# Later, separate plane transposes, feature-major sample outputs, one activation table set and six raw buffers in a streaming-encoder step

## The chip, the cores and the metric

The kernel runs on one core of a Trainium2 chip. The metric is the device time of one execution in microseconds, the median of several runs. The core has a matrix engine (TensorE, PE in the profile; its weight loads are shown apart as PEld), a vector engine (DVE), a scalar engine for activations and copies (ACT), a general engine (POOL) and a sync engine (SP) that here only issues transfers. Each engine works through its own instructions in a fixed order and waits for others by semaphores.

## The reference

One layer of a streaming encoder runs for two groups of rows that share all weights: 256 new positions of a prompt stream, and 64 new positions of a sample stream that has 256 cached positions. D_MODEL is 2048.

```python
xn = rmsnorm(x, norm_mix)
q, k, v, u, vs, g = split(xn @ w_in)            # 8 heads x 128 for q, k, v; 8 groups x 128 for u, vs
# attention, per head and query block, keys of all earlier positions:
z = q @ k.T * 128 ** -0.5
log_stay = where(mask, log_sigmoid(-z), 0)
w = where(mask, exp(log_sigmoid(z) + reverse_cumsum(log_stay) - log_stay), 0)
a = w @ v
bb = gelu(u) * (w_spatial . rmsnorm(gelu(vs)) + b_spatial)
merged = sigmoid(g_a) * (a @ w_branch_a) + sigmoid(g_b) * (bb @ w_branch_b)
h = x + merged @ w_out
y = rmsnorm(h + (silu(gate) * up) @ w_down)     # gate, up = rmsnorm(h) @ w_gate_up, width 5632
```

The outputs are y, the new k and v rows of both groups, and the normalised vs rows of the sample group, all in float32.

## The kernel before

All activations are kept with features on the 128 partitions and the 320 positions (256 prompt, 64 sample) side by side in the free dimension, so one weight tile of 128 by 128 serves both groups. Each float32 product is made of three matmuls in the faster fp32r type (`product`, lines 79 to 84): high half of the weight by high half of x, high by low, low by high. So each weight tile that arrives from HBM is split: `halved` (lines 66 to 72) has ACT cast the raw tile to the high half `wh` (L69) and DVE subtract to get the low half `wl` (L70). Four split tiles (`wsplit`) and three raw tiles (`wraw`) of 128 by 1024 rotate. A call of `weights` (lines 74 to 77) issues one raw transfer of 512 KB on SP's queue and splits it. `block` (lines 86 to 97) makes one output tile of 128 features from all weight tiles of its column, eight k-slices per raw tile, and calls `tick()` after each raw tile: a tick is 24 matmuls.

Work beside the products is put in by ticks: `at(t, fn, p)` runs `fn(p)` when tick t is reached while the program is being written out. A planner then orders the instructions of each engine by this order as priority and by its own estimate of when each is ready; an instruction that it thinks ready early can move ahead on its engine. `tc.keep_in_program_order(ins)` pins one instruction behind whatever was written for its engine just before it. SP's order in the first stage is written by hand.

The stages, in order:

1. Heads 0 and 1 of q, k, v are made k-slice by k-slice, while x is still arriving (lines 169 to 212). Step s needs slices of x from the pair transfers `load_x` (L174) and two raw tiles, one per head, from `load_w` (L178). The raw tiles of this stage lie in a pool of ten, `rpool`, whose memory goes to the attention's pool `apool` afterwards. The normalisation factor `rx` is applied to the results.
2. Heads 2 to 7, six ticks each, k first, then q, then v. Attention runs for a pair of heads at a time, beside these products and those of vs. `attend(p, now)` (lines 380 to 386) sets its steps:
   - `att_scores` (now+1): TensorE makes scores in three PSUM banks of the four `aux` ones; DVE and ACT bring them to the tile `w`; ACT computes Abs, Exp and Ln into `e`, in two parts (L298 to L300).
   - `att_values` (now+1): `turn_begin` splits v into its two planes of 16 bits with four ACT copies (L266, L267) and has ACT issue one DMA transpose (L269).
   - `att_sums` (now+2): DVE does the reverse sums (L307, L311, L313).
   - `att_weights` (now+3): ACT computes Exp on `w` (L318), then for each of the two 16-bit planes a copy (L323) and a DMA transpose on its own queue (L324), from `e` to `c`.
   - `att_join` (now+5): DVE writes the two turned planes together again (L331), and the planes of v (`turn_end`, L277).
   - `att_out` (now+8): TensorE multiplies weights and values (L343 to L351). The prompt's outputs come with features on partitions. The sample's come with positions on partitions, so ACT copies them (`own`, L347) and TensorE transposes them (L353). Then ACT and DVE split the outputs into high and low halves (L357, L358).
   The tiles `w`, `e` and `c` exist once each, so a pair's scores can be written only when the pair before is through with them.
3. vs (eight blocks, Gelu), u (eight blocks), with the spatial gate's steps, which use the same `turn_begin` and `turn_end`.
4. Gates, branch products, w_out, the feed-forward network in three slices, and the last normalisation. The change does not touch these, apart from the first block of gates, up to which the raw tiles of stage 2 are used.

Of the kernel before, what the change touches and what calls it, by code (L numbers as in the profile page):

```python
# [21 lines left out]
HALF = 8  # L22
# [11 lines left out]
def stream_step(ctx: ExitStack, tc: tile.TileContext, xT, w_in, w_a, w_b, w_out, w_gu, w_down,  # L34
                gains, ws_t, bs, ck_t, cv, y_t, k_t, v_t, sv_t):
    nc = tc.nc
    pool = lambda name, bufs=1, **kw: ctx.enter_context(tc.tile_pool(name=name, bufs=bufs, **kw))
    const = pool("const")
    wraw = pool("wraw", 3)
    wsplit = pool("wsplit", 4)  # L40
    big = pool("big")
    tmp = pool("tmp", 2)
# [5 lines left out]
    def aux():  # L48
        return psum.tile([P, 512], F32, tag="aux", bufs=4, name="aux")
# [1 line left out]
    def aux1():  # L51
        return psum.tile([P, 512], F32, tag="aux1", bufs=1, name="aux1")

    state = {"tick": 0}
    later: dict[int, list] = {}

    def at(tick, fn, *a):
        assert tick > state["tick"], (tick, state["tick"])
        later.setdefault(tick, []).append((fn, a))
# [40 lines left out]
    def pair(name, shape=(2, T), dt=F32):  # L100
        return big.tile([P, *shape], dt, tag="D", bufs=24, name=name)
# [21 lines left out]
    ident = const.tile([P, P], F32, name="ident")  # L123
# [48 lines left out]
    def load_x(i):  # L172
        xp[i] = pair("x")
        nc.sync.dma_start(out=xp[i], in_=xT[:, 2 * i : 2 * i + 2, :])  # L174

    def load_w(h, c, n):
        raw = rpool.tile([P, 6 * P], F32, tag="raw1", bufs=10, name="raw1")
# [11 lines left out]
            nc.vector.tensor_tensor(out=squares[0], in0=squares[0], in1=t, op=ALU.add)  # L189

    with tc.manual_schedule(engines={mybir.EngineType.SP}):
        for i in ahead[0]:
            load_x(i)
        for s, (c, n) in enumerate(steps):
            raws = [load_w(0, c, n)]
            for i in ahead.get(s + 1, ()):
                load_x(i)
            raws.append(load_w(1, c, n))
            ws = []
            for h in range(2):  # L200
                ws.append(halved(raws[h], 3 * n))
                if h == 0:
                    for m in range(c, c + n):
                        xs.append(gained(xp[m // 2][:, m % 2, :], g_mix[:, m : m + 1]))
            if s == NS - 1:
                nc.vector.tensor_tensor(out=totx, in0=squares[0][:, 0, :], in1=squares[0][:, 1, :], op=ALU.add)
                got["rx"] = rms("rx", totx, D)
            for h in range(2):
                for b in range(3):
                    for j in range(n):  # L210
                        product(first[h][b], ws[h], n * b + j, xs[c + j], c + j == 0, c + j == KD - 1)
            if 1 <= s < NS - 1:
                square(s - 1)
            if s == NS - 2:
                square(7)
# [9 lines left out]
    nc.gpsimd.memset(mask, 0.0)  # L225
    for i in (0, 2, 3):
# [3 lines left out]
    NA = 9 * P  # L230
# [31 lines left out]
    def turn_begin(t2):  # L262
        hw = t2.bitcast(U16).rearrange("p j (t w) -> p j t w", w=2)
        flat = pair("flat", (2, 5 * P), U16)
        for i in range(2):
            nc.scalar.copy(out=flat[:, i, 0:512].rearrange("p (j t) -> p j t", j=2), in_=hw[:, :, 0:TP, 1 - i])  # L266
# [13 lines left out]
    def att_scores(p):  # L280
        s = attn[p]
        q, k, ck = s["q"], s["k"], s["ck"]
        zb, zc = [aux(), aux()], aux()
        for j in range(2):
            nc.tensor.matmul(zb[j][:, 0:128], q[:, j, 0:128], k[:, j, 0:128], start=True, stop=True)
            nc.tensor.matmul(zb[j][:, 128:384], q[:, j, 128:256], k[:, j, 0:256], start=True, stop=True)
        nc.tensor.matmul(zc[:, 256:384], s["qs"], k[:, :, TP:T], start=True, stop=True)
        for j in range(2):
            nc.tensor.matmul(zc[64 * j : 64 * j + 64, 0:256], s["qs"][:, 64 * j : 64 * j + 64], ck[:, j, :], start=True, stop=True)
        w = s["w"] = apool.tile([P, NA], F32, tag="w", name="w")  # L290
        e = s["e"] = apool.tile([P, NA], F32, tag="e", name="e")
        flat = mask.rearrange("p i t -> p (i t)")
        for j in range(2):
            nc.vector.tensor_tensor(out=w[:, j * 384 : (j + 1) * 384], in0=zb[j][:, 0:384], in1=flat[:, 0:384], op=ALU.add)
        nc.scalar.copy(out=w[:, 768:1024], in_=zc[:, 0:256])
        nc.vector.tensor_tensor(out=w[:, 1024:NA], in0=zc[:, 256:384], in1=flat[:, 384:512], op=ALU.add)
        for r in (slice(0, 768), slice(768, NA)):
            nc.scalar.activation(out=e[:, r], in_=w[:, r], func=AF.Abs)  # L298
            nc.scalar.activation(out=e[:, r], in_=e[:, r], func=AF.Exp, scale=-1.0)
            nc.scalar.activation(out=e[:, r], in_=e[:, r], func=AF.Ln, bias=1.0)  # L300

    def att_sums(p):
        s = attn[p]
# [9 lines left out]
            nc.vector.tensor_tensor(out=w[:, r], in0=w[:, r], in1=c[:, r], op=ALU.subtract)  # L313

    def att_weights(p):
        s = attn[p]
        w = s["w"]
        nc.scalar.activation(out=w, in_=w, func=AF.Exp)  # L318
        hw = w.bitcast(U16).rearrange("p (n w) -> p n w", w=2)
        flat = s["e"].bitcast(U16).rearrange("p (i n) -> p i n", i=2)  # L320
        to = s["c"].bitcast(U16).rearrange("p (i n) -> p i n", i=2)
        for i in range(2):
            nc.scalar.copy(out=flat[:, i, :], in_=hw[:, :, 1 - i])  # L323
            nc.scalar.dma_start_transpose(out=to[:, i, :].rearrange("p (b q) -> p b q", q=P), in_=flat[:, i, :])  # L324

    def att_join(p):
        s = attn[p]
# [9 lines left out]
    def att_out(p):  # L337
        s = attn[p]
        wt, vn, cvt = s["w"].rearrange("p (b q) -> p b q", q=P), s["vn"], s["cv"]
        so, po = aux(), aux()  # L340
        for i in range(2):
            for j in range(2):
                nc.tensor.matmul(so[64 * j : 64 * j + 64, 0:P], wt[:, 6 + i, 64 * j : 64 * j + 64],  # L343
                                 cvt[:, i, j, :], start=i == 0, stop=False, skip_group_check=True)
        nc.tensor.matmul(so[:, 0:P], wt[:, 8, :], vn[:, 4, :], start=False, stop=True, skip_group_check=True)
        own = tmp.tile([P, P], F32, tag="own", bufs=1, name="own")
        nc.scalar.copy(out=own, in_=so[:, 0:P])  # L347
        for j in range(2):
            nc.tensor.matmul(po[:, j * 256 : (j + 1) * 256], vn[:, 2 * j, :],
                             wt[:, 3 * j : 3 * j + 2, :], start=True, stop=False)  # L350
            nc.tensor.matmul(po[:, j * 256 + 128 : (j + 1) * 256], vn[:, 2 * j + 1, :],  # L351
                             wt[:, 3 * j + 2, :], start=False, stop=True)
        nc.tensor.transpose(so[:, P : 2 * P], own, ident)  # L353
# [56 lines left out]
    for g in range(H):  # L410
        ps = block(w_in[4 * H + g], xs)
        t = t320("ev")
# [51 lines left out]
    for g in range(H):  # L464
        ps = block(w_in[3 * H + g], xs)
        t = t320("ev")
# [5 lines left out]
    for m in range(KD):  # L472
        gate = []
        for i in range(2):
            ps = block(w_in[5 * H + i * KD + m], xs)
            t = t320("ev")
# [21 lines left out]
    for m in range(KD):  # L498
        x = t320("xr")
# [50 lines left out]
    ms, r, e = (const.tile([P, 3], F32, name=f"col{i}") for i in range(3))  # L550
# [70 lines left out]
```

## Time and profile before

| | us |
|---|---|
| median of three runs | 1748.37 |
| lowest, highest | 1747.83, 1749.90 |
| the profiled execution: its time | 1749.64 |
| the profiled execution: its span on the core | 1747.8 |
| mean granted clock of TensorE | 0.991 |

The span is what the trace covers; all starting times in rows of the trace are counted from its begin. In a row of the timeline stand start, length, engine, line, operation, output and inputs, shapes and count; in square brackets the engine's idle time before it and what ended that. "ACTq" and "SPq" are the time in which the engine's sequencer issues a transfer. A matmul in float32 is shown as two instructions. A row of the stretches gives for each engine the busy time and the number of instructions, then the mean granted clock of TensorE (1.00 is full), the share of the DMA engines' time, and what they moved.

### The profile page before, as it was taken

The page shows a single profiled execution, that of the slowest core. Times are in us where ns is not written, and L with a number is a line of the kernel's source. Part 1 is how long each engine was busy: PE and PEld are TensorE (multiplying, and loading weights), DVE is VectorE, ACT ScalarE, POOL GpSimd, SP SyncE. Part 2 cuts the span into 40 slices and gives each one's busy share as a digit, 9 for nine tenths or more (in the row PEclk, how much of TensorE's full clock was granted, in tenths as well). Part 3 has the DMA queues.
Part 4 walks back from the last instruction along what each step waited for, and adds up shares of the span by engine and source line. Part 5 has one row for each costly group of instructions (what it writes and reads, how often), then busy time and mean ns, then how long its engine had stood idle before and what let it go on. Part 6 is the DMA issues. An engine that isn't in the chain of part 4 may idle for free.

```text
span 1747.8 us, 27345 instructions
## 1 busy us (share of the span) xinstructions
PE 1705.2 (98%) x11542; PEld 1696.4 (97%) x11542; DVE 868.8 (50%) x1079; ACT 675.9 (39%) x837; POOL 57.4 (3%) x93
## 2 busy tenths in 40 slices
PE   9989889999999999999999999999999999999997
PEld 8878889999999999999999999999999999999996
DVE  6545455654444444555444444444444444444555
ACT  6643464433333333444333333233333322333342
POOL 0200001000000000220000000000000000000000
PEclk9999999999999999999999999999999999999998
DMA  7766554655444444554544455454444554444453
GB/s 242 177 162 168 146 144 139 166 153 152 149 147 155 146 152 152 174 174 149 152 150 147 153 147 153 149 150 151 147 153 148 149 153 146 155 146 151 131 151 110
DMA packets 100059, 268.30 MB, mean 154 GB/s; under 512 B 28992, under 2 KB 36160, under 8 KB 99936
## 3 DMA queue, kind: packets, MB, share of 16 engines
q1 hardware_dynamic: 77040, 252.74, 47.4%
q10 hardware_dynamic: 20112, 5.03, 2.3%
q0 software_dynamic: 2784, 8.79, 1.8%
q8 instruction: 90, 1.47, 0.4%
q14 instruction: 33, 0.27, 0.0%
HBM read 256.03 MB, written 5.51 MB: 150 GB/s over the span
## 4 chain that ended last, share of the span: by engine, by line
PE 90%; DMA 3%; ACT 3%; DVE 2%; issue 1%; ACTq 1%; SPq 0%; DVEq 0%
PE acc L82 29%; PE acc L84 29%; PE acc L83 29%; DMA raw<-w_in 2%; DMA c<-e 2%; ACT wh L69 1%; PE aux L82 0%; PE aux L83 0%; PE aux L84 0%; DVE wl L70 0%; ACTq L269 0%; ACT e L323 0%; DVE c L311 0%; DVE h L560 0%; ACTq L324 0%
## 5 line engine op out<-in xcount | busy, mean ns | idle before, releaser
L69 ACT CAST wh<-raw 128x1024 fp32r<-128x1024 f32 (+2 forms) x486 | 497.7, 1025 | 1004.3 <-PE acc L83 766.2
L70 DVE TENSOR_TENSOR wl<-raw,wh 128x1024 fp32r<-128x1024 f32 (+2 forms) x486 | 580.0, 1195 | 504.0 <-ACT wh L69 503.4
L84 PE MATMUL acc<-A,wl 128*128 128x320 f32 x2496 | 775.5, 311 | 11.3 <-DVE wl L70 11.3
L82 PE MATMUL acc<-A,wh 128*128 128x320 f32 x2496 | 777.1, 311 | 3.7 <-ACT wh L69 3.7
L83 PE MATMUL acc<-A,wh 128*128 128x320 f32 x2496 | 774.4, 310 | 0.0
L84 PEld LDWEIGHTS acc<-A,wl 128*128 128x128 f32 x2496 | 471.5, 189 | 12.7 <-DVE wl L70 12.5
L82 PEld LDWEIGHTS acc<-A,wh 128*128 128x128 f32 x2496 | 472.1, 189 | 6.7 <-ACT wh L69 4.9
L83 PEld LDWEIGHTS acc<-A,wh 128*128 128x128 f32 x2496 | 471.6, 189 | 0.2
L84 PE MATMUL acc<-act,wl 128*128 128x320 f32 x704 | 217.5, 309 | 0.0
L82 PE MATMUL acc<-act,wh 128*128 128x320 f32 x704 | 217.5, 309 | 0.0
L83 PE MATMUL acc<-act,wh 128*128 128x320 f32 x704 | 217.5, 309 | 0.0
L82 PEld LDWEIGHTS acc<-act,wh 128*128 128x128 f32 x704 | 132.1, 188 | 0.0
L83 PEld LDWEIGHTS acc<-act,wh 128*128 128x128 f32 x704 | 132.1, 188 | 0.0
L84 PEld LDWEIGHTS acc<-act,wl 128*128 128x128 f32 x704 | 132.1, 188 | 0.0
L82 PE MATMUL acc<-mh,wh 128*128 128x320 f32 x256 | 79.1, 309 | 0.0
L83 PE MATMUL acc<-ml,wh 128*128 128x320 f32 x256 | 79.1, 309 | 0.0
L84 PE MATMUL acc<-mh,wl 128*128 128x320 f32 x256 | 79.1, 309 | 0.0
L521 DVE TENSOR_TENSOR bb<-acc,rh 128x320 f32<-128x320 f32 x44 | 21.6, 491 | 57.5 <-PE acc L84 57.5
L518 DVE TENSOR_TENSOR ev<-acc,rh 128x320 f32<-128x320 f32 x44 | 21.6, 491 | 56.4 <-PE acc L84 56.3
L534 DVE TENSOR_TENSOR h<-acc,h 128x320 f32<-128x320 f32 x48 | 23.5, 489 | 49.9 <-PE acc L84 49.9
L82 PEld LDWEIGHTS acc<-mh,wh 128*128 128x128 f32 x256 | 48.0, 188 | 0.0
L83 PEld LDWEIGHTS acc<-ml,wh 128*128 128x128 f32 x256 | 48.0, 188 | 0.0
(182 smaller groups left out, 1095.1 us busy)
## 6 DMA issues: line engine op xcount, KB each, us to landing
raw<-w_gu SPq DMA_DIRECT2D x176, 512.0 KB, 3.7
raw<-w_in SPq DMA_DIRECT2D x132, 512.0 KB, 3.8
raw<-w_down SPq DMA_DIRECT2D x80, 512.0 KB, 3.6
raw<-w_out SPq DMA_DIRECT2D x32, 512.0 KB, 3.9
raw<-w_a SPq DMA_DIRECT2D x16, 512.0 KB, 3.6
raw<-w_b SPq DMA_DIRECT2D x16, 512.0 KB, 3.5
raw<-w_in SPq DMA_DIRECT2D x14, 384.0 KB, 9.1
raw<-w_down SPq DMA_DIRECT2D x16, 256.0 KB, 2.7
```

Of the source, the lines that this page charges most:

```text
L69: nc.scalar.copy(out=wh[:, : n * P], in_=raw[:, : n * P])
L70: nc.vector.tensor_tensor(out=wl[:, : n * P], in0=raw[:, : n * P], in1=wh[:, : n * P].bitcast(F32), op=ALU.subtract)
L82: nc.tensor.matmul(ps[:, :T], a, x[0], start=first, stop=False)
L83: nc.tensor.matmul(ps[:, :T], a, x[1], start=False, stop=False)
L84: nc.tensor.matmul(ps[:, :T], b, x[0], start=False, stop=last)
L518: nc.vector.tensor_tensor(out=t, in0=pg, in1=got["rh"], op=ALU.mult)
L521: nc.vector.tensor_tensor(out=u, in0=pu, in1=got["rh"], op=ALU.mult)
L534: nc.vector.tensor_tensor(out=hs[m], in0=ps, in1=hs[m], op=ALU.add)
```

## The change

- **Sample's outputs.** In `att_out` values are now the stationary operand and weights the moving one, so that the sample's outputs come with features on partitions like the prompt's. The copy `own` and the transpose go. The sample's part is made and split first.
- **Activation tables.** In `att_scores` Abs, Exp and Ln each run over all 1152 columns at once; for the first and the last pair a table set that holds Exp and Ln both is loaded ahead, pinned.
- **Planes.** `att_weights` now computes Exp and turns plane 0; `att_plane(p, 1)`, two ticks later, turns plane 1. Exp and the planes' copies are pinned, and so is the first copy of `turn_begin`. The steps of `attend` move to now+1 (scores), +3 (sums), +5 (values), +8 (weights, plane 0), +10 (plane 1), +11 (join), +12 (out).
- **Raw buffers.** From the opening of the attention's pool until the first gates, every other call of `weights`, beginning with the first one, takes its raw tile from three further buffers in that pool.
- **x.** The first pair of x comes in two transfers, with head 0's first weights between them, and the other pairs are issued later: one pair in each of steps 1, 2, 3, 5 and 6, two in step 4.

```diff
     def weights(src, n):
-        raw = wraw.tile([P, HALF * P], F32, tag="raw", name="raw")
+        state["n"] += 1
+        if state["more"] is not None and state["n"] % 2:
+            raw = state["more"].tile([P, HALF * P], F32, tag="raw2", bufs=3, name="raw2")
+        else:
+            raw = wraw.tile([P, HALF * P], F32, tag="raw", name="raw")
...
-    ahead = {0: (0,), 1: (1,), 2: (2,), 3: (3, 4), 4: (5, 6), 5: (7,)}
+    ahead = {1: (1,), 2: (2,), 3: (3,), 4: (4, 5), 5: (6,), 6: (7,)}
...
-        for i in ahead[0]:
-            load_x(i)
+        load_x(0, ((0, 1),))
         for s, (c, n) in enumerate(steps):
             raws = [load_w(0, c, n)]
-            for i in ahead.get(s + 1, ()):
+            if s == 0:
+                load_x(0, ((1, 2),))
+            for i in ahead.get(s, ()):
                 load_x(i)
             raws.append(load_w(1, c, n))
...
+    state["more"] = apool
...
         for i in range(2):
-            nc.scalar.copy(out=flat[:, i, 0:512]..., in_=hw[:, :, 0:TP, 1 - i])
+            c = nc.scalar.copy(out=flat[:, i, 0:512]..., in_=hw[:, :, 0:TP, 1 - i])
+            if i == 0:
+                tc.keep_in_program_order(c)
...
-        for r in (slice(0, 768), slice(768, NA)):
-            nc.scalar.activation(out=e[:, r], in_=w[:, r], func=AF.Abs)
-            nc.scalar.activation(out=e[:, r], in_=e[:, r], func=AF.Exp, scale=-1.0)
-            nc.scalar.activation(out=e[:, r], in_=e[:, r], func=AF.Ln, bias=1.0)
+        if p in (0, 3):
+            tc.keep_in_program_order(nc.scalar.preload_act_table_set("natural_log_exp_and_others"))
+        nc.scalar.activation(out=e, in_=w, func=AF.Abs)
+        nc.scalar.activation(out=e, in_=e, func=AF.Exp, scale=-1.0)
+        nc.scalar.activation(out=e, in_=e, func=AF.Ln, bias=1.0)
...
     def att_weights(p):
-        nc.scalar.activation(out=w, in_=w, func=AF.Exp)
+        w = attn[p]["w"]
+        tc.keep_in_program_order(nc.scalar.activation(out=w, in_=w, func=AF.Exp))
+        att_plane(p, 0)
+
+    def att_plane(p, i):
...
-        for i in range(2):
-            nc.scalar.copy(out=flat[:, i, :], in_=hw[:, :, 1 - i])
-            nc.scalar.dma_start_transpose(out=to[:, i, :]..., in_=flat[:, i, :])
+        tc.keep_in_program_order(nc.scalar.copy(out=flat[:, i, :], in_=hw[:, :, 1 - i]))
+        nc.scalar.dma_start_transpose(out=to[:, i, :]..., in_=flat[:, i, :])
...
-        for i in range(2):
-            for j in range(2):
-                nc.tensor.matmul(so[64 * j : 64 * j + 64, 0:P], wt[:, 6 + i, 64 * j : 64 * j + 64],
-                                 cvt[:, i, j, :], start=i == 0, stop=False, skip_group_check=True)
-        nc.tensor.matmul(so[:, 0:P], wt[:, 8, :], vn[:, 4, :], start=False, stop=True, skip_group_check=True)
-        own = tmp.tile([P, P], F32, tag="own", bufs=1, name="own")
-        nc.scalar.copy(out=own, in_=so[:, 0:P])
+        nc.tensor.matmul(so[:, 0:P], vn[:, 4, :], wt[:, 8, :], start=True, stop=True, skip_group_check=True)
+        for j in range(2):
+            for i in range(2):
+                nc.tensor.matmul(so[:, 64 * j : 64 * j + 64], cvt[:, i, j, :], wt[:, 6 + i, 64 * j : 64 * j + 64],
+                                 start=False, stop=True, skip_group_check=True)
...
-        nc.tensor.transpose(so[:, P : 2 * P], own, ident)
-        for src, r in ((po, slice(0, TP)), (so[:, P : 2 * P], slice(TP, T))):
+        for src, r in ((so[:, 0:P], slice(TP, T)), (po, slice(0, TP))):
...
     def attend(p, now):
         at(now + 1, att_scores, p)
-        at(now + 1, att_values, p)
-        at(now + 2, att_sums, p)
-        at(now + 3, att_weights, p)
-        at(now + 5, att_join, p)
-        at(now + 8, att_out, p)
+        at(now + 3, att_sums, p)
+        at(now + 5, att_values, p)
+        at(now + 8, att_weights, p)
+        at(now + 10, att_plane, p, 1)
+        at(now + 11, att_join, p)
+        at(now + 12, att_out, p)
...
         if m == 0:
+            state["more"] = None
             att_ctx.close()
```

More of the change, by code (lines that the diff above doesn't have):

```diff
@@ L52, in aux1 @@
         return psum.tile([P, 512], F32, tag="aux1", bufs=1, name="aux1")
-    state = {"tick": 0}
+    state = {"tick": 0, "n": 0, "more": None}
     later: dict[int, list] = {}
@@ L170, in stream_step, with load_x @@
     rpool = raw_ctx.enter_context(tc.tile_pool(name="first", bufs=1))
-    def load_x(i):
-        xp[i] = pair("x")
-        nc.sync.dma_start(out=xp[i], in_=xT[:, 2 * i : 2 * i + 2, :])
+    def load_x(i, parts=((0, 2),)):
+        if i not in xp:
+            xp[i] = pair("x")
+        for a, b in parts:
+            nc.sync.dma_start(out=xp[i][:, a:b, :], in_=xT[:, 2 * i + a : 2 * i + b, :])
     def load_w(h, c, n):
@@ L265, in turn_begin @@
         for i in range(2):
-            nc.scalar.copy(out=flat[:, i, 0:512].rearrange("p (j t) -> p j t", j=2), in_=hw[:, :, 0:TP, 1 - i])
+            c = nc.scalar.copy(out=flat[:, i, 0:512].rearrange("p (j t) -> p j t", j=2), in_=hw[:, :, 0:TP, 1 - i])
+            if i == 0:
+                tc.keep_in_program_order(c)
             nc.scalar.copy(out=flat[:, i, 512:640].rearrange("p (j t) -> p j t", j=2), in_=hw[:, :, TP:T, 1 - i])
@@ L315, in att_weights @@
     def att_weights(p):
+        w = attn[p]["w"]
+        tc.keep_in_program_order(nc.scalar.activation(out=w, in_=w, func=AF.Exp))
+        att_plane(p, 0)
+    def att_plane(p, i):
         s = attn[p]
-        w = s["w"]
-        nc.scalar.activation(out=w, in_=w, func=AF.Exp)
-        hw = w.bitcast(U16).rearrange("p (n w) -> p n w", w=2)
+        hw = s["w"].bitcast(U16).rearrange("p (n w) -> p n w", w=2)
         flat = s["e"].bitcast(U16).rearrange("p (i n) -> p i n", i=2)
         to = s["c"].bitcast(U16).rearrange("p (i n) -> p i n", i=2)
-        for i in range(2):
-            nc.scalar.copy(out=flat[:, i, :], in_=hw[:, :, 1 - i])
-            nc.scalar.dma_start_transpose(out=to[:, i, :].rearrange("p (b q) -> p b q", q=P), in_=flat[:, i, :])
+        tc.keep_in_program_order(nc.scalar.copy(out=flat[:, i, :], in_=hw[:, :, 1 - i]))
+        nc.scalar.dma_start_transpose(out=to[:, i, :].rearrange("p (b q) -> p b q", q=P), in_=flat[:, i, :])
     def att_join(p):
```

## The prediction

> **What bounds the kernel now.** I read the page's engine table first, then TensorE's waits, then busy time by stretch, then the two queues that TensorE was found to wait for.
>
> ```profile
> span 1747.8 us, 27345 instructions
> PE 1705.2 (98%) x11542; PEld 1696.4 (97%) x11542; DVE 868.8 (50%) x1079; ACT 675.9 (39%) x837; POOL 57.4 (3%) x93
> ```
>
> TensorE is busy for 98% of the span, so other engines' work counts only where TensorE is idle or slow because of it. Its waits, longest in total first (who waited for whom: us, times, longest):
>
> ```profile
> PE aux L353 <- ACT own L347: 13.5, 4, 4.8
> PE acc L84 <- DVE wl L70: 11.3, 4, 5.4
> PE acc L82 <- ACT wh L69: 3.7, 5, 1.0
> ```
>
> Where they lie (columns: stretch, its length, busy time and count of PE, PEld, DVE, ACT, POOL, granted clock, DMA share, GB/s):
>
> ```profile
> 0.00:20.00 20.00, 16.26 (x93) 14.90 (x94) 11.06 (x19) 13.38 (x24) 0.89 (x8) 1.00 0.86 258
> 60.00:80.00 20.00, 16.02 (x108) 15.20 (x107) 10.65 (x18) 15.63 (x17) 1.80 (x3) 1.00 0.75 152
> 80.00:100.00 20.00, 14.58 (x82) 13.93 (x83) 7.14 (x9) 5.33 (x6) 1.11 (x2) 0.83 0.85 142
> 100.00:120.00 20.00, 17.21 (x108) 16.95 (x107) 7.35 (x9) 6.75 (x12) 1.08 (x2) 0.91 0.49 158
> 140.00:160.00 20.00, 16.82 (x116) 15.90 (x115) 10.24 (x13) 7.14 (x10) 1.11 (x2) 1.00 0.64 177
> 180.00:200.00 20.00, 17.71 (x119) 17.15 (x117) 13.61 (x20) 9.28 (x9) 0.57 (x1) 1.00 0.52 112
> 200.00:220.00 20.00, 16.80 (x107) 16.19 (x106) 7.47 (x10) 6.29 (x9) 0.54 (x1) 0.91 0.54 173
> 240.00:260.00 20.00, 14.84 (x103) 14.14 (x102) 10.21 (x12) 10.27 (x14) 2.13 (x2) 0.94 0.71 178
> 256.00:260.00 4.00, 0.32 (x2) 0.32 (x3) 1.30 (x3) 1.58 (x3) 0.00 (x0) 0.68 0.85 246
> 260.00:280.00 20.00, 20.00 (x125) 20.00 (x125) 7.49 (x9) 7.46 (x12) 2.84 (x3) 0.89 0.39 121
> 400.00:440.00 40.00, 40.00 (x275) 40.00 (x274) 19.12 (x23) 14.89 (x18) 0.00 (x0) 1.00 0.50 148
> ```
>
> The seven 20-us rows from 60 to 260 us hold 26.0 us of idle TensorE (the lengths less the busy times: 4.0, 5.4, 2.8, 3.2, 2.3, 3.2, 5.2). These are the four rounds of attention, one per pair of heads. The clock comes on top: 20 us times one less the granted clock gives 3.4, 1.8, 1.8, 1.2 and 2.2 us in the five rows below 1.00, 10.4 us; some 1.3 us of that fell on idle time (256 to 260 us: 0.32 of a clock for 4 us), so **9 us** were lost by working at half clock after a stall. The row at 400 us is the undisturbed pace: 275 matmuls in 40 us, 24 of them (one block of eight weight tiles, a "tick") in 3.5 us.
>
> What makes TensorE run dry is seen in the first round on ACT and DVE:
>
> ```profile
> 79.04 2.21 ACT L323 COPY e<-w 128x1152 uint16<-128x1152 uint16 x2
> 80.22 6.21 ACTq L324 DMA_TRANSPOSE c<-e  x2
> ...
> 98.36 1.04 ACT L69 CAST wh<-raw 128x1024 fp32r<-128x1024 f32 x1 [5.43 <-DMA raw<-w_in]
> ...
> 92.11 0.82 DVE L331 COPY w<-c 128x1152 uint16<-128x1152 uint16 x1 [10.81 <-DMA c<-e]
> 92.82 1.21 DVE L70 TENSOR_TENSOR wl<-raw,wh 128x1024 fp32r<-128x1024 f32 x1
> ```
>
> ACT issues both turned planes in a row and its queue is shut for 6.2 us. DVE then stands 10.8 us at the join (L331) with the low halves of the weights (L70) queued behind it. While L70 stands, no raw buffer comes free, so after the join the three raw buffers refill from nothing, and ACT waits 5.4 us for one (98.36). The split weights run only four tiles ahead, one of them in use: about three ticks, 10.5 us, and that is what 10.8 us of DVE and then a raw load use up. The wait of L353 is the same drought in another place: the copy that the transpose needs is on ACT behind that cast.
>
> **The change, part by part.** *Planes apart, later, pinned.* The turned planes are issued two ticks apart (weights at +8, second plane at +10, join at +11, out at +12, where it was +3, +3, +5, +8). How long one takes:
>
> ```profile
> L324 ACTq DMA_TRANSPOSE c<-e x2: 1704/2721/3738, 135.4 to 137.2; - x2
> DMA to landing us min/median/max: 5.8/6.2/6.5
> ```
>
> In the second round the first issue held ACT for 1.7 us and the second, right behind it, 3.7. Apart, I take 1.7 to 3.7 us each. On ACT the longest stretch without a weight cast then becomes Exp and copy (some 1.2 and 1.1 us) and one issue, 4.0 to 6.0 us, against 10.5 us of lead: nothing. On DVE the second plane lands 5.8 to 6.5 us after issue and the join stands one tick (3.5 us) later in program order, so DVE waits 0 to 3 us with L70 behind it, again inside the lead. What out needs: from ACT's arrival at the second plane, copy 1.1, landing 6.5, two joins of 0.82 and two copies of v, some 10 us; TensorE reaches out two ticks plus ACT's lead of three after that, 17.5 us. Nothing lands on TensorE while the lead holds; rivals one and three are what it costs if not.
>
> *Six raw buffers.* Every other weight tile of this stage comes from a second pool of three. A slow load of about 10 us (three ticks) is now behind six ticks of raw data instead of three, 21 us. It has one price: the new pool lies where the first stage's raw buffers were, and the very first tile of head 2 uses it.
>
> ```profile
> 42.80 0.53 POOL L225 MEMSET mask<- 128x512 f32 x1 [41.30 <-DVE wl L70]
> ...
> 43.55 1.05 ACT L69 CAST wh<-raw 128x1024 fp32r<-128x1024 f32 x1 [1.80 <-PE aux L83]
> ...
> raw<-w_in SPq DMA_DIRECT2D x132, 512.0 KB, 3.8
> ```
>
> The neighbouring tile in that memory could be written only at 42.8 us. A load issued then lands 3.8 us later, at 46.6, where the cast now starts at 43.55; with 1.05 for the cast it is ready at 47.7. TensorE ends the first stage at about 48 to 50 us (288 matmuls of 0.146 us from 5.85 us, and 2 us of waits). The cover is 0.3 to 2.3 us; between no cost and 2 us I take 0.5.
>
> *One table set, single passes.*
>
> ```profile
> L300 ACT ACT_TABLE_LOAD x5 | 6.4, 1283 | 0.1
> L318 ACT ACT_TABLE_LOAD x4 | 5.1, 1283 | 0.1
> L299 ACT ACT_TABLE_LOAD x2 | 2.6, 1283 | 0.0
> ```
>
> Eleven loads of 1.28 us become two or three, and 24 activations 12 longer ones. Some 11 us come off ACT, at 39%, so by itself it is worth nothing; in the first round it lets ACT catch up before the 4 us stall that ends 79.8. That stall is in the 26.0 already. Likewise moving att_sums to +3 and turning v at +5 costs nothing while that work has four to ten ticks before its reader.
>
> *Sample's outputs on rows.* The transpose (L353) and its copy go; products change shape.
>
> ```profile
> 98.80 0.66 PE L343 MATMUL aux<-cv,w 128*64 128x128 f32 x8
> 99.39 0.49 PE L345 MATMUL aux<-rows,w 128*128 128x128 f32 x2
> ...
> 100.15 0.38 PE L351 MATMUL aux<-w,rows 128*128 128x128 f32 x2
> 100.37 0.60 PE L349 MATMUL aux<-w,rows 128*128 128x256 f32 x2
> ...
> 103.97 0.47 PE L353 MATMUL aux<-ident,own 128*128 128x128 f32 x1 [2.79 <-ACT own L347]
> ```
>
> The transpose costs at most 0.47 us a round. The eight of L343 take 0.59 us now (98.80 to 99.39), 0.074 each, with 64 columns loaded and 128 moved; after, 128 loaded and 64 moved. L351 passes 128 by 128 in 0.11 (100.15 to 100.37, two). So they cost between half of 0.074 and 0.11 each: from 0.3 us less to 0.3 us more a round. I take nothing, and 0.15 us for the transpose: **0.5 us** in four rounds. The Trainium skill (TensorE: Matmul & The Clock Gate, LDWEIGHTS) has a weight load cost its columns over 1.2 GHz, whatever is moved; 128 columns would be 107 ns, an estimate from that page of 0.26 us a round lost, and the sum 1 us worse. The row of L351 agrees with that pace; no run here shows a 64-wide move yet.
>
> *x one step ahead.* First stage waits:
>
> ```profile
> 5.85 0.41 PE L82 MATMUL acc<-A,wh 128*128 128x320 f32 x1 [0.76 <-ACT wh L69]
> 8.19 0.41 PE L82 MATMUL acc<-A,wh 128*128 128x320 f32 x1 [0.76 <-ACT wh L69]
> 12.90 0.41 PE L82 MATMUL acc<-A,wh 128*128 128x320 f32 x1 [0.48 <-ACT wh L69]
> 16.66 0.42 PE L82 MATMUL acc<-A,wh 128*128 128x320 f32 x1 [0.74 <-ACT wh L69]
> ```
>
> They sum to 2.7 us. At 258 GB/s a pair of x (320 KB) takes 1.2 us; 160 KB fewer stand ahead of the first weights (0.6 us), 320 KB fewer ahead of the next three, 640 KB fewer ahead of the sixth. All four shrink: **2.0 us**, between 0 (SP has one issue more) and 2.7. From about 20 us the stage is TensorE's, and every x still stands one step ahead.
>
> **The sum.** Idle 26.0, half clock 9, start 2.0, products 0.5: 37.5. I give back 3: 0.5 for the new pool, and 2.5 for out and the next scores, which now stand at one tick or the same one and want five of four aux buffers, about 0.6 us a round for the cast and subtraction that free one. Net 34.5. The profiled execution took 1749.64 us (span 1747.8 and 1.84 around it): 1715.1. It ran 1.27 us above the median of the three runs, 1748.37, so the forecast is **1714 us**.
>
> The clock's 9 us is weighed against a rule, since it decides what small stalls left over would cost.
>
> ```profile
> 104.00:106.00 2.00, 2.00 (x8) 2.00 (x9) 1.81 (x3) 0.67 (x2) 0.00 (x0) 0.50 0.11 39
> 106.00:108.00 2.00, 2.00 (x12) 2.00 (x11) 0.00 (x0) 0.00 (x0) 0.00 (x0) 0.69 0.75 246
> ```
>
> After the 2.79 us wait that ended at 103.97 the clock was 0.50 and then 0.69, 1.6 us lost. The Trainium skill (TensorE: Matmul & The Clock Gate, What's actually happening) drops the clock after an idle window of about 3.4 us; by that only the waits of 4.0, 5.4 and 4.8 us would count, an estimate of 5 us, and the forecast 1718. The row shows a drop after less, so 9 stands.
>
> **Rivals.** *One: the second plane still holds DVE.* Join is not pinned and stands one tick behind the second issue. If that lands as late as in the first round (from 80.22 to 92.11, 11.9 us), DVE waits 8.4 us and works 1.6 more on the joins (0.82 each); the lead less a cast and a subtraction (1.04 and 1.21) is 8.2. TensorE stops for some 2 us a round and runs at half clock after (1.6, as after the wait that ended at 103.97): four times 3.6 is 14 or 15, **1729 us**. For it: every round had its DVE wait there; against it: the second round's 6.5 us, and raw data for six ticks behind it.
>
> *Two: the drought only moves.* L353's wait hides that the next product would have waited for the same late raw tile, so if the planner sets the planes together again or the turned traffic still slows raw loads, only the start (2.0) and the transposes (0.5) come off: **1746 us**. Against it: the pins hold the copy of a plane behind the cast of its own tick.
>
> *Three, slower: out itself waits.* Out stands one tick behind the join, three before. If ACT reaches the second plane with its lead spent, the cover is two ticks, 7 us, against copy 1.1, landing 11.9 and joins of 2.7, 15.7: 8.7 us a round and 1.6 of half clock, four times 10.3, 41 us in place of the 37.5 gained: **1752 us**. It decides from a landing near 12 us with no lead at all; one alone isn't enough.
>
> **How the numbers follow.** Forecast 0.68, rival one 0.20, two 0.06, three 0.06. The forecast's own range is 1707 (nothing given back, a little more at the products and the start) to 1721 (the pool 2, the products 1, no start, some stall left). For 8 in 10 it must reach rival one: 1706 to 1731. Three runs lay within 0.12%, so under 0.2% is no change: 1745 to 1752. Faster 0.88, same 0.06, slower 0.06.
>
> **What would show it.** No row of TensorE waiting for own; waits for wl and wh in 60 to 280 us under 3 us; granted clock 1.00 in all those stretches; DVE's join waits under 3 us each; two or three table loads in the score lines; first-stage waits near 0.7 us. I am wrong if TensorE waits at the out products, if the clock still drops in a round, or if DVE stands over 8 us at the join.

## The result and the profile after

The changed kernel took 1718.3 us (median of four runs, 1718.07 to 1720.44) where the kernel before took 1748.78 on the same chip: a ratio of 0.9828, with a 95% interval of 0.9811 to 0.9845. The forecast was 1714. The profiled execution took 1718.36 us, with a span of 1716.6: 31.2 us less than before.

The page's head and TensorE's waits after (who waited for whom: us, times, longest); the lines L86 to L88 are the products that were L82 to L84:

```profile
span 1716.6 us, 27308 instructions
PE 1696.8 (99%) x11538; PEld 1691.7 (99%) x11538; DVE 867.5 (51%) x1079; ACT 664.9 (39%) x813; POOL 57.0 (3%) x93
...
PE aux L299 <- DMA ck<-ck_t: 4.0, 1, 4.0
...
PE acc L86 <- ACT wh L69: 1.2, 2, 0.9
...
PE acc L88 <- DVE wl L70: 0.3, 1, 0.3
```

The waits for `own` (13.5 us) are gone, and of those for low halves (11.3) 0.3 us is left. A new one has come: 4.0 us for the cached keys. By stretch (columns as before):

```profile
0.00:20.00 20.00, 17.56 (x102) 16.49 (x103) 11.25 (x18) 13.39 (x23) 0.89 (x8) 1.00 0.87 258
...
38.00:40.00 2.00, 2.00 (x16) 2.00 (x15) 0.73 (x1) 0.46 (x1) 0.00 (x0) 1.00 0.01 4
...
40.00:60.00 20.00, 19.58 (x130) 18.86 (x128) 12.94 (x18) 8.56 (x10) 8.42 (x21) 1.00 0.74 237
60.00:80.00 20.00, 16.45 (x101) 16.09 (x102) 12.02 (x19) 10.90 (x14) 3.30 (x6) 0.91 0.67 215
80.00:100.00 20.00, 20.00 (x139) 20.00 (x138) 11.03 (x13) 8.51 (x9) 1.09 (x2) 1.00 0.88 227
```

Between 40 and 260 us TensorE was idle for 4.0 us (0.42 and 3.55 in two rows, nothing in the rest), where it had been 26.0. The clock is below full in one row, 0.91, 1.8 us in place of some 9. The turned planes in the first round, on ACT and DVE:

```profile
80.87 1.15 ACT L336 COPY e<-w 128x1152 uint16<-128x1152 uint16 x1
82.05 2.07 ACTq L337 DMA_TRANSPOSE c<-e  x1
84.21 1.05 ACT L69 CAST wh<-raw 128x1024 fp32r<-128x1024 f32 x1 [2.19 <-PE acc L88]
85.16 1.15 ACT L336 COPY e<-w 128x1152 uint16<-128x1152 uint16 x1
86.34 1.33 ACTq L337 DMA_TRANSPOSE c<-e  x1
...
88.50 0.83 DVE L344 COPY w<-c 128x1152 uint16<-128x1152 uint16 x1 [1.98 <-DMA c<-e]
92.22 0.83 DVE L344 COPY w<-c 128x1152 uint16<-128x1152 uint16 x1 [1.39 <-DMA c<-e]
...
125.23 5.06 ACTq L337 DMA_TRANSPOSE c<-e  x1
...
138.61 0.85 DVE L344 COPY w<-c 128x1152 uint16<-128x1152 uint16 x1 [4.32 <-DMA c<-e]
```

In the first round a cast stands between the two issues, each issue shuts ACT for 1.3 to 2.1 us instead of 6.2 in a row, and DVE waits 2.0 and 1.4 us at the join where it waited 10.8. The second round (the last two rows) was worse: one issue took 5.1 us and the join waited 4.3. Over all four rounds DVE stood 14.2 us at the join, where it had stood 29.8, and 10.7 us at the planes of v (3.6 before). None of this reached TensorE. In the first round, out's first product stands 11 us behind the end of the join:

```profile
104.50 0.38 PE L354 MATMUL aux<-w,rows 128*128 128x128 f32 x2
```

The account closes: idle time 22 us less, half clock 7.2, the end of the first stage 1.4 us earlier (the sum of x's squares reaches TensorE at 44.77 us, it was 46.14), and 0.6 us left for the products and rounding: 31.2.

**The new wait.** The cached keys of the first pair, POOL's issue and TensorE's product with them:

```profile
56.47 0.18 POOL L226 COPY ck<-rx 128x1 f32<-128x1 f32 x1 [3.20 <-DVE rx L134]
56.95 0.56 POOL L246 DMA_DIRECT2D ck<-ck_t  x1
...
63.55 0.65 PE L299 MATMUL aux<-ck,qs 128*64 128x256 f32 x4 [3.97 <-DMA ck<-ck_t]
```

In the kernel before the same issue stood at 55.27 us and the product at 60.62, without a wait:

```profile
55.27 0.56 POOL L238 DMA_DIRECT2D ck<-ck_t  x1
...
60.62 0.65 PE L289 MATMUL aux<-ck,qs 128*64 128x256 f32 x4
```

The transfer is released by the norm factor `rx`. It was issued 1.7 us later than before, landed after about 6.5 us, and TensorE was at the scores over a microsecond sooner (57.78 against 59.00). Why `rx` is late begins in the row of 38 us: the DMA engines stand still (0.01 of their time, 4 GB/s). The first weight tile of head 2 goes to a new raw buffer in the first stage's memory and waits until 41.4 us, with the whole queue of loads behind it; ACT's casts of this stage, which began at 43.55, begin at 45.84, and the catching up on ACT and DVE is mixed with the steps of `rx`.

```profile
41.39 38.61 SPq L80 DMA_DIRECT2D raw<-w_in  x12
...
45.84 2.00 ACT L69 CAST wh<-raw 128x1024 fp32r<-128x1024 f32 x2 [5.46 <-PE aux L138]
```

### The profile page after: what moved, and what is told of

Read it like the earlier page. It is cut to its first block, busy times and chain, and to the rows that moved or that the text cites. A ratio compares the mean times of both kernels' runs of the same rounds, so it can differ in the third digit from the quotient of the medians.

```text
span 1716.6 us, 27308 instructions
## 1 busy us (share of the span) xinstructions
PE 1696.8 (99%) x11538; PEld 1691.7 (99%) x11538; DVE 867.5 (51%) x1079; ACT 664.9 (39%) x813; POOL 57.0 (3%) x93
## 4 chain that ended last, share of the span: by engine, by line
PE 97%; DVE 1%; DMA 1%; issue 0%; ACT 0%; SPq 0%; POOL 0%; DVEq 0%
PE acc L86 32%; PE acc L88 32%; PE acc L87 32%; PE aux L87 0%; PE aux L88 0%; PE aux L86 0%; DMA raw<-w_in 0%; DMA ck<-ck_t 0%; DVE h L572 0%; PE aux L360 0%; PE aux L452 0%; PE aux L357 0%; DVE wl L70 0%; PE aux L296 0%; PE aux L299 0%
## 5 line engine op out<-in xcount | busy, mean ns | idle before, releaser
L86 PE MATMUL acc<-A,wh 128*128 128x320 f32 x2496 | 774.1, 310 | 1.2 <-ACT wh L69 1.2
L88 PE MATMUL acc<-A,wl 128*128 128x320 f32 x2496 | 772.2, 309 | 0.3 <-DVE wl L70 0.3
L86 PEld LDWEIGHTS acc<-A,wh 128*128 128x128 f32 x2496 | 469.3, 188 | 3.5 <-ACT wh L69 1.7
L88 PEld LDWEIGHTS acc<-A,wl 128*128 128x128 f32 x2496 | 469.2, 188 | 0.8 <-DVE wl L70 0.7
L88 PE MATMUL acc<-act,wl 128*128 128x320 f32 x704 | 217.5, 309 | 0.0
L86 PE MATMUL acc<-act,wh 128*128 128x320 f32 x704 | 217.5, 309 | 0.0
L86 PEld LDWEIGHTS acc<-act,wh 128*128 128x128 f32 x704 | 132.2, 188 | 0.0
L88 PEld LDWEIGHTS acc<-act,wl 128*128 128x128 f32 x704 | 132.2, 188 | 0.0
L86 PE MATMUL acc<-mh,wh 128*128 128x320 f32 x256 | 79.1, 309 | 0.0
L88 PE MATMUL acc<-mh,wl 128*128 128x320 f32 x256 | 79.1, 309 | 0.0
L86 PEld LDWEIGHTS acc<-mh,wh 128*128 128x128 f32 x256 | 48.0, 188 | 0.0
```

Source lines behind the costliest of these rows:

```text
L86: nc.tensor.matmul(ps[:, :T], a, x[0], start=first, stop=False)
L88: nc.tensor.matmul(ps[:, :T], b, x[0], start=False, stop=last)
```

## The experiments

All times are medians beside runs of the kernel before on the same chip; the chips differ (before: 1748.8, 1745.1, 1745.7 and 1746.2 in the four sets), so ratios are compared, or times within a set.

| run | us | ratio to before, 95% interval |
|---|---|---|
| after (first set) | 1718.3 | 0.9828 [0.9811, 0.9845] |
| c1, cached keys released early | 1713.27 | 0.9816 [0.9801, 0.9831] |
| c2, old raw buffers first | 1714.21 | 0.9817 [0.9802, 0.9832] |
| b2, rows alone | 1729.64 | 0.9915 [0.9897, 0.9933] |
| a1, three raw buffers | 1712.87 | 0.9811 [0.9794, 0.9827] |
| after (third set) | 1719.24 | 0.9846 [0.9830, 0.9863] |
| c3, c1 and c2 | 1713.11 | 0.9812 [0.9797, 0.9826] |
| a2, planes together | 1727.41 | 0.9903 [0.9872, 0.9934] |
| a3, old times | 1743.89 | 0.9978 [0.9963, 0.9993] |
| b3, rows and times alone | 1714.20 | 0.9814 [0.9800, 0.9829] |
| a5, old tables | 1718.52 | 0.9841 [0.9826, 0.9855] |
| a6, old times, three raw buffers | 1739.12 | 0.9959 [0.9944, 0.9973] |
| a7, no pins | 1717.44 | 0.9834 [0.9817, 0.9850] |

### The one stall left

c1, on the kernel after:

```diff
         if p == 0:
-            gated(s["ck"][:, 0, 0:1])
+            nc.gpsimd.tensor_copy(s["ck"][:, 0, 0:1], totx[:, 0:1])
```
(and the same for the cached values)

> The kernel after, but the first pair's cached keys and values are released by the sum of squares of x (ready about 34 us) and not by the norm factor rx (56 us), so that their transfer falls into the stretch from 36 to 41 us in which the DMA engines moved under 50 GB/s. Theory (the one stall left, 4.0 us for the cached keys at 63.5 us, and the half clock behind it, some 1.8 us, come from that late transfer): no wait at L299 in the first round, clock 1.00 there, 1718.3 less 5.8, about 1712.5. Rival (the transfer then stands in the way of the first raw tiles, or the scores wait for q and k as long): 1717 to 1719, with a wait of another name near 60 us.

c2, on the kernel after:

```diff
-        if state["more"] is not None and state["n"] % 2:
+        if state["more"] is not None and state["n"] > 3 and state["n"] % 2:
```

> The kernel after, but the first three weight tiles of the attention stage take the three old raw buffers, which are free early, and only the ones behind them alternate with the three new ones. Theory (the first of the new buffers waits for the first stage's memory until 41 us, all loads stand behind it on SP's queue, and the catching up that follows makes rx, the cached keys' release and their transfer late): DMA busy again between 30 and 41 us, casts as before from 43.5 us, rx some 1.5 us earlier, the wait at L299 1 to 2.5 us in place of 4.0, 1714 to 1716.5. Rival (TensorE is simply earlier at the scores, and the cached keys always come at the same distance behind rx): the wait stays near 4 us, 1718.

c3 makes both edits.

> The kernel after with the first three tiles in the old raw buffers and the first pair's cached keys and values released by the sum of squares of x. Theory (each of the two alone had already removed the one stall): no more than either, 4 to 6 us under the kernel after on the same chip. Rival (they add up, since the early loads also shorten the way to rx): over 6 us.

The longest wait of TensorE for weights that is left in c1, and in c2 the end of `rx`, the issue of the cached keys and the product with them:

```profile
PE acc L88 <- DVE wl L70: 0.5, 2, 0.3
...
51.63 0.49 DVE L134 SCALAR_TENSOR_TENSOR rx<-bb,rx 128x320 f32<-128x320 f32 x1
52.66 0.56 POOL L246 DMA_DIRECT2D ck<-ck_t  x1
...
58.94 0.65 PE L299 MATMUL aux<-ck,qs 128*64 128x256 f32 x4
```

Beside waits under 0.5 us and those at the kernel's start and end, nothing remains in either run, and the granted clock is 1.00 in every stretch from 0 to 300 us. Each edit alone removes the whole stall, also c2, which leaves the release at `rx` as it was: more than the 1.5 to 3 us that I expected of it. There `rx` came not 1.5 us earlier but 4.3 (its last step at 51.63, in the kernel after at 55.92), and the cached keys were issued 4.3 us earlier with it. Together the two edits do no more: 6.1 us under the kernel after in their set (1713.11 to 1719.24, ranges apart); in that set's profile of the kernel after the wait was 3.3 us, and the clock of 0.83 in its stretch cost 3.4 more. So the cause of the wait is the late start of all loads behind the handed-over buffer; the release at `rx` matters only because of it. c1, c2, c3, and a1 and b3 below, have the lowest ratios of all, at about 1713 us on chips where before takes 1745 to 1746. For c3 and b3 kernels with the stall ran in the same set and were slower, ranges apart; c1, c2 and a1 are compared by ratio and by trace alone.

### What the parts are worth

b2, on the kernel before, rows alone:

```diff
+        nc.tensor.matmul(so[:, 0:P], vn[:, 4, :], wt[:, 8, :], start=True, stop=True, ...)
+        for j in range(2):
+            for i in range(2):
+                nc.tensor.matmul(so[:, 64 * j : 64 * j + 64], cvt[:, i, j, :], wt[:, 6 + i, 64 * j : 64 * j + 64], ...)
...
-        nc.scalar.copy(out=own, in_=so[:, 0:P])
-        nc.tensor.transpose(so[:, P : 2 * P], own, ident)
```

> The kernel before with one part of the change alone: the sample's outputs with features on rows, without the copy and the transpose. Theory (the 13.5 us at L353 are the same drought that the other waits show: the next product would have waited for the same late weight tile): the wait moves to the low or high halves of the weights, 1744 to 1748. Rival (the transposes' wait is a loss of its own): some 13 us less, 1733 to 1737.

It took 15.5 us off: the rival, and half of the whole change. TensorE's waits for weights there, and the eight new products with the cached values, up to the start of the next:

```profile
PE acc L84 <- DVE wl L70: 9.5, 5, 3.3
...
PE acc L82 <- ACT wh L69: 0.6, 1, 0.6
...
96.17 1.00 PE L344 MATMUL aux<-w,cv 128*128 128x64 f32 x8
97.01 0.65 PE L347 MATMUL aux<-w,rows 128*128 128x256 f32 x2
```

The 13.5 us did not move to another wait; those for low halves fell too, from 11.3 to 9.5. DVE and ACT in the kernel before show why (92.82, a tile, stands with the prediction):

```profile
94.65 2.34 DVE L70 TENSOR_TENSOR wl<-raw,wh 128x1024 fp32r<-128x1024 f32 x2
...
99.44 1.22 DVE L70 TENSOR_TENSOR wl<-raw,wh 128x1024 fp32r<-128x1024 f32 x1 [2.04 <-ACT wh L69]
...
102.71 1.04 ACT L69 CAST wh<-raw 128x1024 fp32r<-128x1024 f32 x1 [3.30 <-DMA raw<-w_in]
103.66 0.26 ACT L347 COPY own<-aux 128x128 f32<-128x128 f32 x1
```

Three tiles had their low halves by 97 us and a fourth by 100.7. TensorE, which had come back at 94.08 and was at out from 98.80, had used about one of them when it stopped for the transpose at 101.2. Weights were there. The copy alone was missing, because on ACT it stood behind the cast of a tile some ticks ahead (at 102.71, not the one at 98.36 that the prediction names), and that cast waited 3.3 us for its load.

b3 is b2 with the new times, and the planes as separate steps; no pins, three raw buffers, old tables, old order of x:

```diff
...
+        at(now + 3, att_sums, p)
+        at(now + 5, att_values, p)
+        at(now + 8, att_weights, p)
+        at(now + 10, att_plane, p, 1)
+        at(now + 11, att_join, p)
+        at(now + 12, att_out, p)
```

> The kernel before with two parts of the change: the sample's outputs on rows, and attention's steps at the new times with the planes as separate steps; no pins, three raw buffers, the old order of x, split passes and single table sets. Theory (rows and times carry the gain, the pins keep the planner from undoing the times, since it takes a transpose for shorter than it is): waits for wl come back in some rounds, 0.986 to 0.991 of before, between the kernel with rows alone (0.9915) and the one with all but the six buffers (0.981). Rival (rows and times are enough): 0.981 to 0.984.

The rival again: 0.9814, 1712.78 to 1714.57 us, below the two kernels of its set with all but one small part of the change (a5 and a7, 1717.15 to 1719.62). Two parts of the change give all that it gives, and the six buffers gave some back. The new times without the rows were not run, so what the times are worth alone isn't known. TensorE's waits in it:

```profile
PE acc L82 <- ACT wh L69: 0.7, 2, 0.5
PE aux L289 <- DMA ck<-ck_t: 0.4, 1, 0.4
PE acc L84 <- DVE wl L70: 0.4, 1, 0.4
```

The other parts, each undone alone on the kernel after. Three raw buffers:

```diff
-    state["more"] = apool
```

> The kernel after with the three raw buffers of before throughout. Theory (it is the planes apart and later that keep DVE and ACT going, and three raw tiles are enough when no one stands for 10 us; the late first loads go too): no waits for wl or wh over 2 us, 1713 to 1718. Rival (the slow raw loads beside a transpose need six ticks of lead): waits for wh in each round, 1722 to 1735.

0.9811, the lowest ratio of all. One wait for low halves of 2.7 us, over the 2 that I had allowed, was left in the profile, which is of the slowest of the four runs (1715.26; the others 1712.28 to 1712.89):

```profile
PE acc L88 <- DVE wl L70: 3.1, 2, 2.7
...
180.00:200.00 20.00, 17.32 (x119) 16.35 (x117) 12.21 (x16) 7.14 (x9) 1.08 (x2) 1.00 0.68 216
```

It costs less than the stall at 63 us that the six buffers bring. Old passes and table loads:

```diff
-        if p in (0, 3):
-            tc.keep_in_program_order(nc.scalar.preload_act_table_set("natural_log_exp_and_others"))
-        nc.scalar.activation(out=e, in_=w, func=AF.Abs)
+        for r in (slice(0, 768), slice(768, NA)):
+            nc.scalar.activation(out=e[:, r], in_=w[:, r], func=AF.Abs)
...
```

> The kernel after with Abs, Exp and Ln in two parts again and no table set loaded ahead. Theory (eleven loads of 1.28 us in place of some four, on an engine that is at 39% and has ten us of lead): within 2 us of the kernel after. Rival (in the first round the loads keep ACT from casting for 10 us, as in the kernel before): a wait of 3 to 5 us for wh or wl near 75 us and half clock behind it, 4 to 7 us over the kernel after.

0.9841, between the two values of the kernel after: nothing, by the ratio (the kernel after was not run in this set). Its longest wait in the rounds is the one for the cached keys; those for low and high halves are 0.7 and 0.2 us in sum:

```profile
PE aux L299 <- DMA ck<-ck_t: 3.5, 1, 3.5
```

The stall that ended at 79.8 us in the kernel before does not return with the old tables. b2, with the old tables and the old times, was still idle for 3.3 us between 60 and 80 us, b3, with the old tables and the new times, for 0.4: it was the later steps that removed it. No pins on Exp, the planes and v:

```diff
...
-        tc.keep_in_program_order(nc.scalar.activation(out=w, in_=w, func=AF.Exp))
+        nc.scalar.activation(out=w, in_=w, func=AF.Exp)
...
-        tc.keep_in_program_order(nc.scalar.copy(out=flat[:, i, :], in_=hw[:, :, 1 - i]))
+        nc.scalar.copy(out=flat[:, i, :], in_=hw[:, :, 1 - i])
```

> The kernel after without the pins on Exp, on the planes' copies and on the first copy of v; the table load stays pinned. Theory (the planner moves Exp and the planes ahead to where it thinks their inputs are ready, so that they stand closer together and nearer to the sums): 4 to 10 us over the kernel after, like the one with the planes together. Rival (the ticks alone set the order): within 2 us of the kernel after.

0.9834: nothing either, again by the ratio. In the first round the planner did move the second plane's copy ahead, as the theory had it, but not the issues into one:

```profile
81.10 2.20 ACT L334 COPY e<-w 128x1152 uint16<-128x1152 uint16 x2
82.28 3.08 ACTq L335 DMA_TRANSPOSE c<-e  x1
85.48 2.84 ACTq L335 DMA_TRANSPOSE c<-e  x1
```

### Planes and times

a2, both planes at +8, the join still at +11:

```diff
-        at(now + 10, att_plane, p, 1)
+        at(now + 8, att_plane, p, 1)
```

> The kernel after with the second plane turned right behind the first again (weights and both planes at +8, join still at +11). Theory (what counts is that the join stands three ticks behind both issues, and ACT's longest stretch without a cast, Exp 1.2, copies 2.2 and issue 6.2, is 9.6 us against 10.5 of lead): within 3 us of the kernel after. Rival (the pair of transposes is what slows raw loads and shuts ACT too long): waits for wh or wl of 2 us or more in each round, 8 to 15 us over the kernel after.

8.2 us over the kernel after in the same set. The profiled execution had one stall more:

```profile
PE acc L88 <- DVE wl L70: 6.2, 3, 5.1
...
180.00:200.00 20.00, 14.88 (x92) 14.62 (x91) 9.75 (x12) 5.24 (x6) 0.54 (x1) 0.91 0.86 203
```

One round of four paid 5.1 us and a half clock behind it, not each one as the rival had it, and not none as the theory had it. There the second issue shut ACT for 7.0 us (at 176.18), and DVE stood 8.1 us at the planes of v and 3.6 at the join, with the low halves behind them. That profile was of 1724.4 us, the fastest of four runs; the others, up to 1735.9, may have paid in more rounds.

a3, the old times with everything else as after, and a6, the same with three raw buffers:

```diff
-        at(now + 3, att_sums, p)
-        at(now + 5, att_values, p)
-        at(now + 8, att_weights, p)
-        at(now + 10, att_plane, p, 1)
-        at(now + 11, att_join, p)
-        at(now + 12, att_out, p)
+        at(now + 1, att_values, p)
+        at(now + 2, att_sums, p)
+        at(now + 3, att_weights, p)
+        at(now + 3, att_plane, p, 1)
+        at(now + 5, att_join, p)
+        at(now + 8, att_out, p)
```

> The kernel after with the old times of attention's steps (values +1, sums +2, weights and both planes +3, join +5, out +8); rows, tables, six raw buffers and the order of x stay as after. Theory (the join behind two planes holds DVE 6 to 11 us, and the low halves behind it run out): DVE waits of 6 us and more at the join in each round, TensorE waits for wl of 4 to 9 us in sum, the clock below 1.00 in two or three stretches, 5 to 12 us over the kernel after. Rival (the transposed copy was the whole loss, and six raw buffers cover the rest): within 2 us of the kernel after.

> The kernel after with the old times of attention's steps and with three raw buffers. Theory (at the old times out stands three ticks behind the join, the join stands at DVE for the second plane, and TensorE waits for it at its first product, whatever the number of raw buffers): waits at the first product of out of 10 us and more in sum, 20 to 28 us over the kernel after, as with six. Rival (the six loads in flight made the transposes late there): the level of rows alone, 8 to 14 us over the kernel after.

a3 gave up 24.7 us of its set's 26.5 (its ten runs lie between 1735.3 and 1746.1), far more than I had expected, and not by low halves. TensorE's waits there:

```profile
PE aux L354 <- DVE w L344: 7.9, 2, 4.9
PE aux L354 <- issue: 6.6, 1, 6.6
PE aux L299 <- DMA ck<-ck_t: 3.3, 1, 3.3
```

and in a6, with DVE's wait at the join in the first round:

```profile
PE aux L353 <- DVE w L343: 9.3, 2, 5.4
PE aux L353 <- issue: 6.7, 1, 6.7
...
87.85 0.81 DVE L343 COPY w<-c 128x1152 uint16<-128x1152 uint16 x1 [11.74 <-DMA c<-e]
```

TensorE stood at out's first product until the join was done. With six raw buffers the gain over before was 1.8 us, with three 7.1; the difference, 5.3, is about what the stall for the cached keys costs, so the wait at out is not the six loads' doing. b2, at the same old times, waited for low halves and not at out, and gained 15.5 us where a6 gained 7.1. Why isn't settled: pins, tables and the order of x stand between the two, and pins and tables are worth nothing at the new times. The turned planes landed later in a6 (median 9.5 us after issue, at most 12.7) than in b2 (7.3 and 9.3); what made them later was not tried.

## Why the prediction was right, and where not

**Right.** The size and its source: idle TensorE and half clock in the four rounds, of which 22.1 of 26.0 and 7.2 of 9 us came back. The join's hold on DVE fell to about 2 us in the first round, no row waits for `own`, and out never waits. Two parts carry it, rows and times: rows alone gained 15.5 us (b2), rows and times as much as the whole change and more (b3). Yet a3, everything but the times, gained only 1.8 us, and a6, with three raw buffers besides, 7.1: less than rows alone, which the prediction doesn't explain.

**Its signs.** Waits for high and low halves between 60 and 280 us were nothing, the first-stage waits fell from 2.7 to 1.4 us (0.7 was forecast), and the eleven table loads became three (L308 twice, L328 once). Two signs were missed. The join's waits were to stay under 3 us and reached 4.3. The clock was to be 1.00 in all stretches and was 0.91 in one, which the prediction counts among the signs of being wrong; but that was behind the wait for the cached keys, not behind a drought of weights.

**The term that was mis-sized** is what is given back: 3 us, of which 2.5 for the aux buffers at out and the next scores, and 0.5 for the new pool. The first was nothing: no round shows a wait there, and in the first the scores follow out's last product at once and their product with cached keys, at 108.55, has no wait:

```profile
106.70 0.38 PE L362 MATMUL aux<-w,rows 128*128 128x128 f32 x2
106.92 0.39 PE L295 MATMUL aux<-k,q 128*128 128x128 f32 x2
...
108.55 0.65 PE L299 MATMUL aux<-ck,qs 128*64 128x256 f32 x4
```

The second was 5.8 us, wait and clock. The prediction saw the mechanism (the first load behind the first stage's memory, late casts) and ended it at the first product of head 2, which did have its cover. It did not ask what else is queued behind those casts: the steps of `rx`, and through its release the cached keys. With 5.8 in place of 3 its own sum gives 1749.64 - 37.5 + 5.8 = 1717.9, against 1718.36 measured for the profiled run. The prediction's other count of the clock, 5 us and 1718, meets the measured time by chance: half clock gave back 7.2 us, and what was missing is the new wait.

**Wrong in its reason, though not in the sum:** "The wait of L353 is the same drought in another place". b2 shows that it was a loss of its own, 15 of 30 us. The sum counted the idle time whatever its name, so that this part came out owes nothing to the reason given; and rival two was priced on that sentence, which would have misled anyone who had to choose one part of the change.

**The smaller terms.** x was put at 2.0 us and is worth about 1.4: the sum of x's squares reached TensorE at 46.14 us in the kernel before, 46.24 in b2 and 46.56 in b3, and between 44.47 and 45.28 us in the kernels with the new order. The products were put at 0.5: the eight new ones take 0.84 us (96.17 to 97.01 in b2), 0.105 each, against 0.59, so 0.25 us a round is lost, near the upper bound, and with the transpose gone the round is about even. The Trainium skill's rule that was weighed there (TensorE: Matmul & The Clock Gate, LDWEIGHTS), a weight load's time as its columns over 1.2 GHz, gives an estimate of 107 ns for 128 columns, and the trace agrees with its 0.105 us. The table sets were put at nothing and are worth nothing (a5). Six raw buffers were put at a cover worth having; a1 and b3 show that with the planes apart none is needed, and the ratios of a1 and of the kernel after differ by 3 to 6 us, the cost of the six as they were laid out.

**The rivals.** One did not come in the kernel after, but a2 is near it: with the planes together the low halves ran out in one round, though behind the planes of v first and then the join. Two is refuted by b2. Three's mechanism is real, TensorE waiting at out for the join, and it is what a3 and a6 show, 14.5 and 16.0 us of waits; it needed the old times and not only a late plane.

## What to carry to other kernels

An operation between two matmuls that sits on an in-order engine behind work for later tiles holds TensorE even when its next operands are ready; find it by asking what stood ahead of the releaser, and remove it first. Put an asynchronous step ahead of the matrix product that needs it by more than its longest seen landing, not its median (here the second plane of the first round was issued 18 us ahead of out, and the longest landing was 13.4); with that done, six buffers, pins and saved table loads had nothing left to do. Before more buffers go in, look whose memory they take, and follow everything that starts late behind the first transfer into it.

## What was not expected of the hardware

The landing of one turned plane (128 by 1152, 16 bits) ranged from 3.2 to 13.4 us after its issue in the kernel after, and to 15.8 in a1, beside ordinary loads. In the kernel after no wait of TensorE came of it; what sets that spread was not tried.

The issue of one such plane shut ACT's queue for 1.3 to 2.6 us in seven of the kernel after's eight, for 5.1 us in the eighth (the row of 125.23) and for 7.0 in one of a2. A neighbouring issue is not the whole of it: in the kernel before, the first transpose of all, of the planes of v at 58.92 us, shut it for 4.2.

After idle TensorE the clock drops by no single length of wait. In the kernel before, the 2.79 us wait that ended at 103.97 was followed by a clock of 0.50, the one of 2.66 us that ended at 152.53 by none below 1.00, and the one of 2.7 us in a1 by none below 1.00 either.
